# Forget gates and scaled keys made in the input projection instead of in the scan

## The chip, the cores and the metric

The kernel runs on one core of a Trainium2 chip. The metric is the device time of one launch in microseconds (us). A core has five engines with a queue each, worked off in order: TensorE (PE; its weight loads are listed apart as PEld), VectorE (DVE), ScalarE (ACT), GpSimd (POOL) and SyncE (SP, which here only issues DMAs). PSUM is the small memory into which TensorE writes; SBUF is the working memory.

## The reference

One layer of a bidirectional encoder over 1024 positions with 1024 channels, all in float32:

```python
h = rmsnorm(x)
proj = h @ w_in                       # 8192 columns
glu_in, q, v, z_f, z_b, og, g_a, g_b = split(proj)
a = silu(layernorm(dwconv31(glu(glu_in)))) @ pw_w
# the HGRN2 scan, once forward (z_f) and once backward (z_b), 8 heads of 128:
f   = lb + (1 - lb) * sigmoid(z)      # forget gate, then clipped to [1e-6, 1]
key = (1 - lb) * sigmoid(-z)
S_t = diag(f_t) S_{t-1} + key_t v_t^T ;  o_t = S_t^T (silu(q_t) * 128**-0.5)
b = (per-head rmsnorm(o_fwd + o_bwd) * silu(og)) @ o_w
x = x + (sigmoid(g_a) * a + sigmoid(g_b) * b) @ w_out
x = x + (silu(dwconv3(h2 @ w_gate)) * (h2 @ w_up)) @ w_down      # h2 = rmsnorm(x)
out = rmsnorm(x)
```

`lb` is a lower bound for each channel and direction, made from `lb_logits`.

## The kernel before

Everything is held transposed: channels on the 128 partitions, positions along the free dimension, in tiles of 128 x 512 ("half" 0 and 1 are the two halves of the sequence). Each float32 product is made of three matmuls on split operands (a high part and a rest, helper `split`, line 125: a cast on ScalarE, a subtraction on VectorE); these are lines 149 to 151. 

TensorE's order is written out by hand, as generators that are advanced piece by piece and woven into each other ("streams"). ScalarE, VectorE, GpSimd and SP get their order from a planner at compile time: it puts ready instructions out by program order under a model of time, and takes buffers of a tag from a pool of fixed size (`bufs`). Only instructions that are pinned keep the program's order. So a change in what the other engines do leaves TensorE's order as it is, and plans the other queues anew.

The parts that matter here, in the order of time:

1. **Input projection.** The columns of q, og, v, z_f, z_b, g_a and g_b are cut into heads of 128 (list `todo`, line 810). Two neighbours of the list are made by one `pair_job` (line 283), a seven-product form of a 2 x 2 block product: the products 1, 2, 6, 7, 5, 4, 3 follow each other on TensorE, 12 matmuls each, in PSUM banks "mm", "tr" and "sc". Products 1, 6 and 7 are copied out by ScalarE (line 440, tile `su`) and TensorE adds the next product but one to the same bank, so it waits for that copy. Four evacuations follow from the sums: for three of the four quadrants VectorE adds two sources (line 800), for the fourth ScalarE copies the bank (line 805); the result lands in an `ev` page (3 buffers) and SP stores it to DRAM (line 806). q and og also get a silu (line 803). Pairs 0 to 7 make q and og, pairs 8 to 18 make v, z_f and z_b of heads 0 to 6 and v of head 7: eight of these eleven pairs hold one z, and pairs 10, 13 and 16 hold z_f and z_b of one head. 19 pairs (`NPAIRS`) run here.
2. Woven into it, in this order: the depthwise convolution, 124 taps on VectorE (line 1039), and the layer norm in two halves (lines 1056 to 1083). Its squares (line 1071) take four `tm` pages at once, of which there are four; its matmuls (lines 1065, 611 and 601) stand in TensorE's order; its silu is line 1079.
3. **The scan.** 16 iterations (8 heads, two halves). `scan_inputs` (line 1152) loads q and the z of both directions and makes from each z the sigmoid of -z (tile `kG`, line 1163), the sigmoid (1164), the gate (1165) and, for both directions at once, the clip (1166). `scan_base` (line 1217) scales the keys (line 1224) and then multiplies keys and queries by products of gates over blocks of 1, 2, 4, ... positions (helper `tt`, line 1144; copies by `woven`, line 1176); `scan_levels` makes the matmuls between blocks (line 1281). The inputs of an iteration are asked for two iterations ahead.
4. TensorE's gaps in the scan are filled with the dense jobs (`rest_jobs`, line 1090): the columns that the 19 pairs leave over, which are z_f and z_b of head 7 (used by the last two iterations), g_a and g_b, and then the convolution's pointwise product. They evacuate through line 803 or 805.
5. Output projections and the feed-forward network follow.

`lbw` (line 981) holds lb and 1 - lb for each head and direction. `ev()` and `tmp()` give the next `ev` or `tm` page.

Of the kernel before, what the change touches and what calls it, by code (L numbers as in the profile page):

```python
# [10 lines left out]
F32 = mybir.dt.float32  # L11
# [3 lines left out]
AF = mybir.ActivationFunctionType  # L15
ALU = mybir.AluOpType
AX = mybir.AxisListType

P = 128
# [29 lines left out]
def tile_hybrid_encoder(  # L49
# [22 lines left out]
    nc = tc.nc  # L72
    PSUM = bass.MemoryType.PSUM
    V, A, G, T = nc.vector, nc.scalar, nc.gpsimd, nc.tensor
# [9 lines left out]
    NH = D // DK  # L84
    OFF_Q, OFF_V, OFF_ZF, OFF_ZB, OFF_OG, OFF_GA, OFF_GB = [2 * CW + i * D for i in range(7)]

    cp = ctx.enter_context(tc.tile_pool(name="const", bufs=1))
# [7 lines left out]
    def nm(s):  # L95
        uid[0] += 1
        return f"{s}_{uid[0]}"
# [3 lines left out]
    def bank(tag):  # L101
        return ps.tile([P, H], F32, tag=tag, name=nm(tag), bufs=BANKS[tag])

    def page(pool, tag, bufs, dt=F32):
        return pool.tile([P, H], dt, tag=tag, name=nm(tag), bufs=bufs)

    def tmp():
        return page(mp, "tm", 4)

    def ev():  # L110
        return page(mp, "ev", 3)
# [439 lines left out]
    def scratch(name, *dims):  # L551
        if not dims:
            return dp.tile([P, H], F32, name=name)
        return [scratch(f"{name}_{i}", *dims[1:]) for i in range(dims[0])]
# [7 lines left out]
    d_q = scratch("d_q", NH, 2)  # L562
    d_v = scratch("d_v", NH, 2)
    d_og = scratch("d_og", NH, 2)
    d_z = scratch("d_z", 2, NH, 2)
    d_bm = scratch("d_bm", NH, 2)
    d_x0 = dp.tile([P, 4, ND, P], F32, name="d_x0")
    d_xt = [[d_x0[:, :, k, :], scratch(f"d_xt_{k}")] for k in range(ND)]
# [227 lines left out]
    def store(dst, func=None):  # L796
        def evac(half, x0, x1=None, op=None):
            t = ev()
            if x1 is not None:
                V.tensor_tensor(t, x0, x1, op=op)  # L800
                x0 = t
            if func is not None:
                A.activation(t, x0, func)
            elif x1 is None:
                A.copy(t, x0)
            nc.sync.dma_start(dst[half], t)

        return evac

    todo = [  # L810
        t
        for h in range(NH)
# [7 lines left out]
        for h in range(NH)  # L820
        for t in (
            (OFF_V + h * DK, store(d_v[h])),
            (OFF_ZF + h * DK, store(d_z[0][h])),
            (OFF_ZB + h * DK, store(d_z[1][h])),
        )
    ]
    todo += [(OFF_GA + i * P, store(d_ga[i], AF.Sigmoid)) for i in range(ND)]
# [153 lines left out]
    lbw = cp.tile([P, 4, 2 * NH], F32, name="lbw")  # L981
# [6 lines left out]
    V.tensor_tensor(lbw[:, 2, :], lbw[:, 1, :], lbw[:, 1, :], op=ALU.subtract)  # L988
    V.tensor_scalar(lbw[:, 3, :], lbw[:, 2, :], -1.0, 1.0, op0=ALU.mult, op1=ALU.add)

    def lb_of(d, h):
        return lbw[:, 2, d * NH + h : d * NH + h + 1]

    def oml_of(d, h):
        return lbw[:, 3, d * NH + h : d * NH + h + 1]
# [143 lines left out]
    hp = tc.alloc_tile_pool(name="heads", bufs=1, reuse_waits="tile")  # L1139
# [3 lines left out]
    def tt(o, a, b, op=ALU.mult):  # L1143
        V.tensor_tensor(o, a, b, op=op)  # L1144

    kscale = cp.tile([P, 2 * NH], F32, name="kscale")
    V.tensor_scalar(kscale, lbw[:, 3, :], DK**-0.5, None, op0=ALU.mult)

    def c4(t):
        return t.rearrange("p (c t) -> p c t", c=4)  # L1150

    def scan_inputs(i):


        h, half = divmod(i, 2)
        q = page(hp, "q", 2)
        f = hp.tile([P, 2, H], F32, tag="f", name=nm("f"), bufs=2)
        kG = hp.tile([P, 2, H], F32, tag="kG", name=nm("kG"), bufs=3)
        nc.sync.dma_start(q, d_q[h][half])
        for d in range(2):  # L1160
            z = page(hp, "zi", 3)
            nc.sync.dma_start(z, d_z[d][h][half])
            A.activation(kG[:, d, :], z, AF.Sigmoid, scale=-1.0)
            A.activation(z, z, AF.Sigmoid)
            A.activation(f[:, d, :], z, AF.Identity, scale=oml_of(d, h), bias=lb_of(d, h))
        V.tensor_scalar(f, f, MIN_FORGET, 1.0, op0=ALU.max, op1=ALU.min)
        return q, f, kG, kscale[:, h : h + NH + 1 : NH]

    def pairs(t, h, other=H):

        return view(t, 0, [[other + h, 2], [2 * h, H // (2 * h)], [1, h]])

    def woven(t, h):

        t_h = page(hp, "A", 8)
        A.copy(pairs(t_h, h, 0), pairs(t, h))  # L1176
        return t_h

    def slot(b, n):
        return b[:, n * P : (n + 1) * P]  # L1180

    def near(t):
        return t.rearrange("p (c t) -> p c t", c=4)

    def over(m):
        return view(m, 0, [[0, 4], [1, 32]])
# [6 lines left out]
    def level(b, A_t, Q_t):  # L1193
        for at, g, o in each():
            T.matmul(b[g, o], A_t[:, at : at + 32], Q_t(at), start=True, stop=True)

    def row(t):
        return lambda at: t[:, at : at + 32]

    def double_keys(kG, tb, h):  # L1200
        n, nb = H // (2 * h), H // h
        tt(pairs(kG, h), pairs(kG, h), view(tb, 1, [[nb - 1, 2], [2, n], [0, h]]))

    def double_queries(qF, q, tb, h):
        n, nb = H // (2 * h), H // h
        tt(pairs(qF, h), q, view(tb, nb + 1, [[-(nb + 1), 2], [2, n], [0, h]]))

    def totals(tb, h, to=None):
        n, nb = H // (2 * h), H // h
        tn = None  # L1210
        if to is None:
            tn = hp.tile([P, 2, n], F32, tag=f"tb{h}", name=nm("tb"), bufs=1 if h < 8 else 2)
            to = view(tn, 0, [[n, 2], [1, n]])
        tt(to, view(tb, 0, [[nb, 2], [2, n]]), view(tb, 1, [[nb, 2], [2, n]]))
        return tn

    def scan_base(ins):


        q, f, kG, ks = ins  # L1220
        qF = hp.tile([P, 2, H], F32, tag="qF", name=nm("qF"), bufs=4)
        D_t = hp.tile([P, 4, 32], F32, tag="D", name=nm("D"), bufs=3)
        for d in range(2):
            V.tensor_scalar(kG[:, d, :], kG[:, d, :], ks[:, d : d + 1], None, op0=ALU.mult)
        k_d, Q1 = page(hp, "A", 8), page(hp, "A", 8)
        tt(k_d, kG[:, 0, :], kG[:, 1, :], ALU.add)
        A1 = woven(kG, 1)
        odd = H // 2
        tt(
            pairs(Q1, 1, 0),  # L1230
            view(q, 0, [[1, 2], [2, odd], [1, 1]]),
            view(f, H, [[1 - H, 2], [2, odd], [1, 1]]),
        )
        tt(
            view(qF, 1, [[H - 1, 2], [2, odd]]),
            view(q, 1, [[-1, 2], [2, odd]]),
            view(f, H + 1, [[-(H + 1), 2], [2, odd]]),
        )
        double_keys(kG, f, 1)
        double_queries(qF, pairs(Q1, 1, 0), f, 1)  # L1240
        tb = totals(f, 1)
        yield
        A2, Q2 = woven(kG, 2), woven(qF, 2)
        double_keys(kG, tb, 2)
        double_queries(qF, pairs(qF, 2), tb, 2)
        tb = totals(tb, 2)
        A4, Q4 = woven(kG, 4), woven(qF, 4)
        yield
        b = bank("sc")
        for n, (k_t, q_t) in enumerate(((k_d, q), (A1, Q1), (A2, Q2), (A4, Q4))):  # L1250
# [154 lines left out]
    class Base:  # L1405
        def __init__(self, ins):
            self.gen, self.val = scan_base(ins), None
# [39 lines left out]
    for h in range(NH):  # L1447
# [4 lines left out]
        for half in range(2):  # L1452
# [3 lines left out]
            ins = scan_inputs(i + 2) if i + 2 < NI else None  # L1456
# [17 lines left out]
            qF, kG = base[:2]  # L1474
# [556 lines left out]
```

## Time and profile before

| | |
|---|---|
| time, median of 3 runs | 1738.62 us (1736.96 to 1738.87) |
| profiled execution | 1740.57 us, its span 1738.7 us |
| granted TensorE clock | 0.997 |
| first store of z | 281.9 us |
| first load of z in the scan | 483.1 us |
| ScalarE table loads | 6 in the whole kernel, one of them (487.7 us) between 122 and 1093 us |

The profile page gives for each engine the time in which it was busy, as a sum and in 40 slices of the span (each 43.5 us, a digit is tenths). PEclk is the granted clock. Groups of instructions are named by line, engine and operation, with out<-in by the program's tile names, the shape and the count; durations are minimum/median/maximum in ns. Waits are told as "who waits <- for whom: us in total, times, longest". A timeline row has the start in us, the duration, and in brackets the idle time of the engine before it and what ended it.

### The profile page before, as it was taken

What the parts mean: (1) busy time and instruction counts of PE and PEld (TensorE: products, weight loads), DVE (VectorE), ACT (ScalarE), POOL (GpSimd) and SP (SyncE); (2) the same over time, 40 slices, a digit from 0 to 9 for tenths busy, and PEclk for the clock granted to TensorE, in tenths of its full rate; (3) what the DMA queues carried; (4) which work ended last, traced back from release to release, by engine and by line L of the source; (5) the groups of instructions that cost most, each with busy time, mean ns of one, the idle gap of its engine ahead of it and who ended that gap; (6) DMA issues with size and microseconds to landing.
All of it is one profiled execution on the core that took longest, in us unless ns stands there. A gap on an engine that the chain in (4) does not pass through costs nothing. (4 is left out here: it accounts for less than half of the span.)

```text
span 1738.7 us, 30440 instructions
## 1 busy us (share of the span) xinstructions
PE 1708.0 (98%) x11806; PEld 1408.5 (81%) x11806; DVE 1252.1 (72%) x1919; ACT 828.3 (48%) x1544; POOL 170.1 (10%) x184
## 2 busy tenths in 40 slices
PE   8999999999999999999999999999999999999997
PEld 6878888887888888888878887888887888888775
DVE  4599999746678888788556467676767776657864
ACT  7444433334476777776342245444334434443333
POOL 2211111100000000000000002011111111000110
PEclk9999999999999999999999999999999999999998
DMA  8768888854663444436579466577777876773842
GB/s 285 241 169 186 199 188 194 212 162 157 210 204 108 126 131 126 126 120 200 178 260 326 140 206 194 146 157 153 163 164 166 178 169 152 241 253 113 199 91 97
DMA packets 343750, 308.26 MB, mean 177 GB/s; under 512 B 25262, under 2 KB 255798, under 8 KB 343606
## 3 DMA queue, kind: packets, MB, share of 16 engines
q1 hardware_dynamic: 289590, 267.51, 48.8%
q0 software_dynamic: 44800, 37.76, 15.0%
q10 hardware_dynamic: 9216, 1.05, 0.4%
q8 instruction: 92, 1.51, 0.4%
q14 instruction: 52, 0.43, 0.1%
HBM read 201.40 MB, written 87.03 MB: 166 GB/s over the span
## 5 line engine op out<-in xcount | busy, mean ns | idle before, releaser
L149 PE MATMUL mm<-hx,wp 128*128 128x512 f32 x1068 | 427.6, 400 | 4.9 <-ACT su L440 2.1
L151 PE MATMUL mm<-hx,wp 128*128 128x512 f32 x1068 | 417.7, 391 | 1.0 <-DVE wp L125 0.8
L150 PE MATMUL mm<-hx,wp 128*128 128x512 f32 x1068 | 416.3, 390 | 0.5 <-DVE hx L125 0.5
L125 ACT CAST wp<-wr 128x1024 fp32r<-128x1024 f32 (+2 forms) x147 | 147.2, 1002 | 272.9 <-PE mm L150 108.0
L149 PEld LDWEIGHTS mm<-hx,wp 128*128 128x128 f32 x1068 | 200.6, 188 | 48.3 <-ACT su L440 3.2
L151 PEld LDWEIGHTS mm<-hx,wp 128*128 128x128 f32 x1068 | 200.4, 188 | 47.2 <-DVE wp L125 4.1
L150 PEld LDWEIGHTS mm<-hx,wp 128*128 128x128 f32 x1068 | 200.8, 188 | 40.9 <-DVE hx L125 1.7
L125 DVE TENSOR_TENSOR wp<-wr,wp 128x1024 fp32r<-128x1024 f32 (+2 forms) x145 | 169.2, 1167 | 84.1 <-ACT wp L125 77.7
L1039 DVE SCALAR_TENSOR_TENSOR acc<-gl,v_b,acc 128x1024 f32<-128x1024 f32 x120 | 148.7, 1273 | 0.4
L1144 DVE TENSOR_TENSOR qF<-qF,tb 128x512 f32<-128x512 f32 x96 | 65.0, 685 | 19.9 <-ACT A L1176 19.8
L440 ACT COPY su<-mm 128x512 f32<-128x512 f32 x82 | 47.5, 580 | 51.8 <-PE mm L151 51.7
L149 PE MATMUL tr<-hx,wp 128*128 128x512 f32 x180 | 70.5, 392 | 0.0
L151 PE MATMUL tr<-hx,wp 128*128 128x512 f32 x180 | 70.1, 389 | 0.0
L150 PE MATMUL tr<-hx,wp 128*128 128x512 f32 x180 | 70.0, 389 | 0.0
L1636 DVE SCALAR_TENSOR_TENSOR tm<-gp,v_a,tm 128x512 f32<-128x512 f32 x88 | 65.9, 749 | 3.8 <-ACT tm L1634 2.0
L125 ACT CAST wq<-sw 128x1024 fp32r<-128x1024 f32 x41 | 43.2, 1053 | 53.5 <-PE mm L150 42.6
L1144 DVE TENSOR_TENSOR kG<-kG,tb 128x512 f32<-128x512 f32 x96 | 65.2, 684 | 3.7 <-PE sc L1281 3.6
L149 PE MATMUL mm<-hy,wp 128*128 128x512 f32 x164 | 64.2, 391 | 0.0
L150 PE MATMUL mm<-hy,wp 128*128 128x512 f32 x164 | 63.8, 389 | 0.0
L150 PE MATMUL sc<-hy,wq 128*128 128x512 f32 x164 | 63.8, 389 | 0.0
L151 PE MATMUL mm<-hy,wp 128*128 128x512 f32 x164 | 63.8, 389 | 0.0
L151 PE MATMUL sc<-hy,wq 128*128 128x512 f32 x164 | 63.8, 389 | 0.0
(372 smaller groups left out, 3571.1 us busy)
## 6 DMA issues: line engine op xcount, KB each, us to landing
wr<-in_w_in_dram SPq DMA_DIRECT2D x48, 512.0 KB
wr<-in_ffn_w_up_dram SPq DMA_DIRECT2D x22, 512.0 KB
sw<-in_w_in_dram SPq DMA_DIRECT2D x38, 256.0 KB
d_g<-ft SPq DMA_DIRECT2D x38, 256.0 KB
sw<-in_ffn_w_up_dram SPq DMA_DIRECT2D x38, 256.0 KB
sw<-in_ffn_w_up_dram POOLq DMA_DIRECT2D x19, 512.0 KB, 8.0
wr<-sw POOLq DMA_DIRECT2D x32, 256.0 KB, 3.8
wr<-wr POOLq DMA_DIRECT2D x32, 256.0 KB, 4.2
```

The source lines that it names most:

```text
L125: parts = A.copy(hi, src), eng.tensor_tensor(lo, src, hi.bitcast(F32), op=ALU.subtract)
L149: T.matmul(acc, whi[:, k, :], ahi, start=first, stop=False, skip_group_check=again)
L150: T.matmul(acc, whi[:, k, :], alo, start=False, stop=False, skip_group_check=again)
L151: T.matmul(acc, wlo[:, k, :], ahi, start=False, stop=last, skip_group_check=again)
L440: A.copy(t, acc)
L1039: V.scalar_tensor_tensor(acc, g[:, k : k + S], tap(k), acc, op0=ALU.mult, op1=ALU.add)
L1144: V.tensor_tensor(o, a, b, op=op)
L1636: V.scalar_tensor_tensor(c, g[:, o + k : o + k + H], vec("fdw", k * NF + j), c, op0=ALU.mult, op1=ALU.add,)
```

## The change

`store_gates` takes the place of `store` for the z columns: after the evacuating addition (or straight from PSUM) it makes both sigmoids, scales the key with (1 - lb) / sqrt(128) on ScalarE, stores it, makes the gate, clips it on VectorE and stores it. DRAM holds `d_f` and `d_k` in place of `d_z`. `scan_inputs` only loads them, and `scan_base` no longer scales the keys. `kscale` is made earlier. TensorE's instructions and their order stay.

```diff
-    d_z = scratch("d_z", 2, NH, 2)
+    d_f = scratch("d_f", 2, NH, 2)
+    d_k = scratch("d_k", 2, NH, 2)
...
+    def store_gates(d, h):
+        def evac(half, x0, x1=None, op=None):
+            f, key = ev(), tmp()
+            if x1 is not None:
+                V.tensor_tensor(f, x0, x1, op=op)
+                x0 = f
+            A.activation(key, x0, AF.Sigmoid, scale=-1.0)
+            A.activation(f, x0, AF.Sigmoid)
+            A.activation(key, key, AF.Copy, scale=kscale_of(d, h))
+            nc.sync.dma_start(d_k[d][h][half], key)
+            A.activation(f, f, AF.Identity, scale=oml_of(d, h), bias=lb_of(d, h))
+            V.tensor_scalar(f, f, MIN_FORGET, 1.0, op0=ALU.max, op1=ALU.min)
+            nc.sync.dma_start(d_f[d][h][half], f)
+
+        return evac
...
-            (OFF_ZF + h * DK, store(d_z[0][h])),
-            (OFF_ZB + h * DK, store(d_z[1][h])),
+            (OFF_ZF + h * DK, store_gates(0, h)),
+            (OFF_ZB + h * DK, store_gates(1, h)),
...
         for d in range(2):
-            z = page(hp, "zi", 3)
-            nc.sync.dma_start(z, d_z[d][h][half])
-            A.activation(kG[:, d, :], z, AF.Sigmoid, scale=-1.0)
-            A.activation(z, z, AF.Sigmoid)
-            A.activation(f[:, d, :], z, AF.Identity, scale=oml_of(d, h), bias=lb_of(d, h))
-        V.tensor_scalar(f, f, MIN_FORGET, 1.0, op0=ALU.max, op1=ALU.min)
-        return q, f, kG, kscale[:, h : h + NH + 1 : NH]
+            nc.sync.dma_start(f[:, d, :], d_f[d][h][half])
+            nc.sync.dma_start(kG[:, d, :], d_k[d][h][half])
+        return q, f, kG
...
-        q, f, kG, ks = ins
+        q, f, kG = ins
...
-        for d in range(2):
-            V.tensor_scalar(kG[:, d, :], kG[:, d, :], ks[:, d : d + 1], None, op0=ALU.mult)
```

More of the change, by code (lines that the diff above doesn't have):

```diff
@@ L989, in tile_hybrid_encoder, with kscale_of @@
     V.tensor_scalar(lbw[:, 3, :], lbw[:, 2, :], -1.0, 1.0, op0=ALU.mult, op1=ALU.add)
+    kscale = cp.tile([P, 2 * NH], F32, name="kscale")
+    V.tensor_scalar(kscale, lbw[:, 3, :], DK**-0.5, None, op0=ALU.mult)
+    def kscale_of(d, h):
+        return kscale[:, d * NH + h : d * NH + h + 1]
     def lb_of(d, h):
@@ L1144, in tt @@
         V.tensor_tensor(o, a, b, op=op)
-    kscale = cp.tile([P, 2 * NH], F32, name="kscale")
-    V.tensor_scalar(kscale, lbw[:, 3, :], DK**-0.5, None, op0=ALU.mult)
     def c4(t):
```

## The prediction

> **What bounds the kernel now.** I read the page first, then the waits of TensorE, then the busy time of each engine in the stages that the change touches.
>
> ```profile
> span 1738.7 us, 30440 instructions
> PE 1708.0 (98%) x11806; PEld 1408.5 (81%) x11806; DVE 1252.1 (72%) x1919; ACT 828.3 (48%) x1544; POOL 170.1 (10%) x184
> PE   8999999999999999999999999999999999999997
> PEclk9999999999999999999999999999999999999998
> ```
>
> TensorE is busy for 98% of the span, at full clock but for the last slice. A change that leaves TensorE's work alone can take away only time in which TensorE waits, or add such time. All waits of TensorE that concern the two touched stages are these (columns: total us, times, longest):
>
> ```profile
> PE mm L149 <- ACT su L440: 2.9, 3, 1.6
> PE sc L1281 <- DVE qF L1144: 1.9, 2, 1.0
> PE mm L149 <- DVE ev L800: 0.9, 1, 0.9
> PE sc L1329 <- ACT kT L1322: 0.7, 1, 0.7
> ```
>
> The scan (lines 1281 and 1329) has 1.9 + 0.7 = 2.6 us of them. That is the ceiling of what the scan can give back. The stages one by one (length, then busy us of each engine with its count, clock, DMA share, GB/s):
>
> ```profile
> core 0: us, PE busy (x) PEld busy (x) DVE busy (x) ACT busy (x) POOL busy (x), PEclk, DMA share, GB/s
> 266.10:324.80 58.70, 57.70 (x254) 47.15 (x253) 58.11 (x56) 18.47 (x26) 9.98 (x9) 1.00 0.83 196
> 324.80:422.30 97.50, 97.50 (x432) 80.20 (x431) 47.87 (x57) 33.81 (x49) 6.31 (x7) 1.00 0.58 162
> 422.30:484.00 61.70, 60.92 (x268) 49.35 (x267) 43.93 (x64) 31.55 (x53) 2.27 (x3) 1.00 0.70 231
> 484.00:500.00 16.00, 16.00 (x72) 13.24 (x71) 10.00 (x18) 13.26 (x22) 0.00 (x0) 1.00 0.81 271
> 500.00:880.00 380.00, 377.29 (x5905) 316.87 (x5904) 297.70 (x651) 261.38 (x596) 14.66 (x16) 1.00 0.45 140
> ```
>
> The rows are pairs 8 to 10 of the projection (with the last convolution taps), pairs 11 to 15, pairs 16 to 18 (with most of the layer norm), the first dense jobs, and the scan. TensorE is full in all of them; the scan's loss is 380.00 - 377.29 = 2.7 us. VectorE is full up to 324.8; ScalarE has half its time free until 484 and is busy for 83% of 484 to 500.
>
> **The change part by part.** Durations come from one profiled execution of 1740.57 us (span 1738.7 and 1.9 around it); it is 0.11% above the median of 1738.62, on which I put the differences.
>
> ```profile
> L1163 ACT ACTIVATE kG<-zi x32: 614/634/660, 489.0 to 800.5; 128x512 f32<-128x512 f32 x32
> L1164 ACT ACTIVATE zi<-zi x32: 614/632/652, 490.1 to 801.3; 128x512 f32<-128x512 f32 x32
> L1165 ACT ACTIVATE f<-zi,lbw x32: 801/814/859, 491.1 to 802.1; 128x512 f32<-128x512 f32 x32
> L1166 DVE TENSOR_SCALAR f<-f x16: 677/693/695, 492.7 to 803.0; 128x1024 f32<-128x1024 f32 x16
> L1224 DVE TENSOR_SCALAR kG<-kG,kscale x32: 469/481/488, 489.7 to 801.1; 128x512 f32<-128x512 f32 x32
> L806 SPq DMA_DIRECT2D d_z<-ev x32: 319/328/1187, 281.9 to 508.8; - x32
> L1162 SPq DMA_DIRECT2D zi<-d_z x32: 319/320/1148, 483.1 to 774.2; - x32
> L440 ACT COPY su<-mm x82: 560/587/590, 116.7 to 1481.9; 128x512 f32<-128x512 f32 x82
> L805 ACT COPY ev<-mm x15: 565/579/582, 286.0 to 508.1; 128x512 f32<-128x512 f32 x15
> ```
>
> *Taken from the scan.* ScalarE loses 32 x (0.634 + 0.632 + 0.814) = 66.6 us, VectorE 16 x 0.693 + 32 x 0.481 = 26.5 us. TensorE gains from this only where it waited. One of the two waits on VectorE shows the cause:
>
> ```profile
> 757.57 0.69 DVE L1166 TENSOR_SCALAR f<-f 128x1024 f32<-128x1024 f32 x1 [0.22 <-ACT f L1165]
> 763.05 0.69 PE L1281 MATMUL sc<-qF,kG 128*64 128x64 f32 x16 [0.90 <-DVE qF L1144]
> ```
>
> The clip with the wait ahead of it takes 0.69 + 0.22 = 0.91 us of a VectorE queue that the matmul then awaits for 0.90. Without clip and scaling I count both of these waits as gone (-1.9) and the ScalarE one (0.7) as gone at even odds (-0.35): **-2.25**, between 0 (the new order of the queues puts others in their place) and -2.6.
>
> *Put into the projection.* 32 halves of z get one chain each: two sigmoids, a scaled copy and an affine step on ScalarE, a clip on VectorE, a second store. The chain is 0.63 + 0.63 + about 0.65 (bound by 0.587 without and 0.814 with two pointer operands) + 0.81 = 2.7 us when each waits for the last; back to back each starts some 0.1 sooner (below, two activations take 1.15), so 2.4. The 11 halves that leave PSUM through the plain copy (7 in pairs, 4 in dense jobs) save 0.58 each. ScalarE's sum is 32 x 2.4 - 11 x 0.58 = 70 us. A product of a pair lasts 2.72 us (97.50 us for 432 matmuls, 12 each), and a pair has seven. A pair with one z half-head has two chains, a pair with both directions (10, 13 and 16) four: 9.6 us of 19. With the 33.81 / 97.50 = 35% that ScalarE has there already, that is some 85% of such a pair and 60% of the others. Hence, outside the layer norm, no queue grows: what waits behind a chain is the copy of a product (line 440), which is due one product later: 2.72 - 0.59 = 2.1 us of room against a backlog of about 1. I cost it at nothing; if the chains came three in a row ahead of such a copy, each further 2.4 us would go straight to TensorE.
>
> *Layer norm on top (422 to 484).* Here is the price. ScalarE has 31.55 of 61.70 us; pairs 16 to 18 add 4 + 2 + 2 chains less two or three plain copies, about 18 us, and the tables change between silu (layer norm) and sigmoid. Together 31.55 + 18 + loads of about 5 is 55 of 61.7, and one wait is already here:
>
> ```profile
> 428.53 1.15 ACT L1079 ACTIVATE cx<-cx 128x512 f32<-128x512 f32 x2 [2.26 <-DVE cx L1078]
> ...
> 433.42 0.62 ACT L125 CAST ch<-cx 128x512 fp32r<-128x512 f32 x1
> 433.95 0.58 ACT L440 COPY su<-mm 128x512 f32<-128x512 f32 x1
> 434.58 0.50 PE L149 MATMUL mm<-hy,wq 128*128 128x512 f32 x1 [0.78 <-ACT su L440]
> 473.35 0.57 ACT L440 COPY su<-mm 128x512 f32<-128x512 f32 x1
> 475.72 0.59 ACT L440 COPY su<-sc 128x512 f32<-128x512 f32 x1 [1.28 <-PE sc L151]
> 478.89 2.66 ACT L125 CAST hx<-tm 128x512 fp32r<-128x512 f32 x4 [2.59 <-PE sc L150]
> ```
>
> A burst of silus and casts from 428.53 makes the copy, and TensorE behind it, late by 0.78. What a table load costs, the trace shows at 30.7 us:
>
> ```profile
> 30.48 0.22 ACT L750 ACTIVATION_READ_ACCUMULATOR junk<-xt 128x1 f32 x1
> 30.72 1.28 ACT L851 ACT_TABLE_LOAD   x1
> 32.02 0.60 ACT L851 ACTIVATE tm<-mm 128x512 f32<-128x512 f32 x1
> 117.32 1.28 ACT L985 ACT_TABLE_LOAD   x1
> 119.48 0.22 ACT L985 ACTIVATE lbw<-su 128x16 f32<-128x16 f32 x1 [0.88 <-DVE su L984]
> ```
>
> 1.28 us, with nothing before or after it. The load at 117.32 ran ahead of a wait and so was hidden, so a load in front of the burst costs 0 to 1.28; I take **+1.3**, since the queue is full there. The pair's four chains then end about 0.3 behind the room of the next pair's first copy: **+0.3** (0 to 3). At 475.72 the copy of a product would stand behind one chain and one load that begin after 473.9: 473.9 + 1.28 + 2.4 + 0.5 = 478.1 instead of 476.3; it is due 2.72 after its product ended, at 475.7 + 2.7 = 478.4. Shifted by the burst's own load it is 1.0 late: **+1.1** (0 to 3.7, one chain and one load). The casts at 478.89 have 2.59 of idle time ahead that covers them; if that is gone they push the second halves of the first dense jobs by what exceeds it.
>
> [...]
>
> *VectorE and PSUM.* 28 clips of half the size of line 1166 (0.35 to 0.48) go into the projection, eight of them ahead of 324.8 where VectorE is full and where the evacuation of line 800 already holds TensorE up once by 0.9: **+0.4**, one clip (0 to 1.8, half of them in the way). Elsewhere it is half idle and they cost nothing. The plain-copy halves keep their bank for two sigmoids, 0.5 us longer; "mm" has three banks and the next product uses another, so nothing.
>
> *DMAs and queues.* 32 more stores and 32 more loads of 256 KB. Eight more stores to 324.8 are 2.1 MB in 58.7 us, 36 GB/s on 196 with a share of 0.83, still under 1; later there is more room. SP issues 64 more at 0.33 us (21 us over 600). A store waits in SP's queue for its chain, and weight loads wait behind it, by 2 to 3 us; these loads run a pair, 19 us, ahead. In the scan f and the keys come straight from DMA; an iteration lasts some 23 us (380 / 16), a load is issued an iteration ahead, so nothing; the start of the scan loses the three activations between load and first multiply and loads twice as much, which I set against each other. POOL's queue is not passed.
>
> **Sum:** -2.25 + 1.3 + 0.3 + 1.1 + 0.4 = +0.85 us, +0.9 us or 0.05%: 1738.62 + 0.9 = 1739.5.
>
> **The rivals.** *Slower: the queue of ScalarE overflows in the layer norm.* The place is 422 to 484. The four "tm" buffers now hold key tiles as well, and the four squares of the layer norm need all four at once; ScalarE stands at 55 of 61.7 us. From a backlog of 2.1 us on (the room of a product's copy), every further microsecond is TensorE's. A backlog of 5 us in each half of the layer norm gives 2 x (5 - 2.1) = 5.8 us, to the other terms: +6.7, 1745.3; with 8 us in each, +12.7, 1751. For it: the wait of 0.78 at 434.58 without any of the new work. Against it: 6 us of free time over the stretch, and stores that nobody awaits.
>
> [...]
>
> *Faster: the scan gives more than its waits.* If the denser queues also slow TensorE between the waits that the profile names, relieving ScalarE of 66.6 of 261 us and VectorE of 26.5 of 298 could return more: all 2.7 us of the scan's loss, the 0.9 and 0.8 in the projection through another order, and about as much again unseen: -4.4 to -6, 1733 to 1734. For it: nothing but that ends of matmuls are modelled. Against it: PEld is 316.87 / 380 = 83% in the scan and 80.20 / 97.50 = 82% where nothing waits, so the scan is as tight as the rest. [...]
>
> *Nothing is moved in effect:* the planner puts chains into idle time and the scan's waits stay: 0 to +1, inside my forecast.
>
> **How the numbers follow.** About 0.2% (3.5 us) is what a measurement of this kernel can tell from no change. My sum with its bounds stays inside this in 0.49. The overflow has 0.32 and counts as slower; the drain has 0.06, and lies on the border, I count it slower too. Faster has 0.13. The likeliest case's own range is 1736 to 1742. The range for 8 in 10 leaves out half of the faster case and the far end of the overflow: 1735 to 1750.
>
> **What would show it.** Right: TensorE's waits at line 1281 on VectorE gone or halved; five ScalarE table loads between 270 and 490 where there was one; ScalarE over 85% in 422 to 484 and some 17 us less per 100 in the scan; TensorE's waits on line 440 grown by 2 to 4 us in that stretch, nothing new in pairs 9 to 15. Wrong: waits of TensorE on the layer norm's matmuls (lines 611 and 601), which would be the buffers' doing; waits on weights (line 125), which would be SP's queue; or new waits in the scan or after it, where a new order of the queues would have done what I did not foresee.

## The result, and the profile after

The change makes the kernel slower: 1757.01 us (median of 4 runs, 1756.31 to 1758.77) against 1738.74 us for the kernel before in 4 runs alongside, a ratio of 1.0101 with a 95% interval of 1.0087 to 1.0115. The forecast of 1739.5 and its range, up to 1750, missed it. The profiled execution took 1757.49 us, its span 1755.7, which is 17.0 more than before.

The page of the kernel after, its head, TensorE's slices and its clock:

```profile
span 1755.7 us, 30563 instructions
PE 1715.3 (98%) x11806; PEld 1412.7 (80%) x11806; DVE 1242.1 (71%) x1903; ACT 850.4 (48%) x1569; POOL 172.5 (10%) x184
PE   8999999999999999999999999999999999999997
PEclk9999999999999999999999999999999999999999
```

At this resolution almost nothing has moved: the span is 17.0 longer and TensorE, with the same 11806 matmuls, is busy 7.3 longer. The stages show where. The five rows answer to the five stage rows of the prediction (pairs 8 to 10, 11 to 15, 16 to 18, first dense jobs, scan; each bound is moved by what the same matmul is late there). The others, behind the "...", follow the granted clock, which is the first number behind the five busy times:

```profile
267.84:328.72 60.88, 59.01 (x254) 48.39 (x253) 57.70 (x59) 34.19 (x50) 10.02 (x9) 0.97 0.85 201
328.72:434.21 105.49, 101.43 (x432) 82.57 (x431) 55.76 (x73) 61.76 (x96) 6.31 (x7) 0.97 0.67 196
434.21:500.69 66.48, 61.82 (x268) 49.10 (x267) 44.05 (x68) 51.96 (x83) 2.23 (x3) 1.00 0.63 211
500.69:521.46 20.77, 17.73 (x72) 12.93 (x71) 13.70 (x23) 13.98 (x23) 0.00 (x0) 1.00 0.93 303
521.46:901.46 380.00, 376.96 (x5906) 317.12 (x5905) 274.38 (x606) 217.84 (x516) 16.95 (x16) 1.00 0.52 165
...
98.00:102.00 4.00, 4.00 (x12) 3.14 (x11) 3.39 (x6) 1.51 (x3) 0.75 (x5) 0.57 0.31 104
314.00:315.00 1.00, 1.00 (x3) 0.77 (x3) 1.00 (x2) 0.26 (x1) 0.43 (x1) 0.50 0.49 100
422.70:430.00 7.30, 7.25 (x22) 6.05 (x23) 2.08 (x3) 2.23 (x5) 1.24 (x2) 0.53 0.10 36
```

The four stages ahead of the scan last 253.6 us with 1026 matmuls; before, the same matmuls took 233.9 us. The loss is there: 19.7 us. In the scan ScalarE gave up 261.38 - 217.84 = 43.5 us and VectorE 297.70 - 274.38 = 23.3, and TensorE's idle time went from 2.7 to 3.0.

TensorE's waits in the stages ahead of the scan, and its largest of the scan (from the waits of the whole run):

```profile
PE mm L149 <- ACT su L440: 4.9, 4, 1.9
PE ob L612 <- DVE tm L1076: 2.8, 1, 2.8
PE mm L149 <- ACT hx L125: 1.8, 2, 0.9
PE ob L602 <- ACT tm L601: 1.8, 1, 1.8
PE ob L1088 <- DVE tm L1076: 1.1, 2, 0.9
PE mm L150 <- DVE hx L125: 1.1, 3, 0.7
...
PE sc L1295 <- DVE qF L1167: 2.9, 4, 1.3
```

These six make 13.5 us, where before there were 0.9 + 0.8 = 1.7: 11.8 of the 19.7. The other 8 us are TensorE being busy for longer with the same work. Most of that is the clock: in the profile after it stood at 0.50 for three windows of 3.4 us within these stages (one from 313.6, two from 422.8), each counted, by that clock, as half a window's work lost: 3 x 1.7 = 5.1 us. The rest, about 3, is not taken apart here; the first matmuls after the waits are a part of it (0.5 to 0.6 us instead of 0.39 in the rows below).

TensorE executes the same matmuls in the same order in both kernels, so the start of the same matmul can be compared in two traces. Against before, in us gained or lost in each stage (worked out from the two traces; minus is faster):

| | until 262 us | pairs 8-10 | 11-15 | 16-18 | first dense | scan | after it |
|---|---|---|---|---|---|---|---|
| after | +1.9 | +2.6 | +7.6 | +4.8 | +4.8 | -0.2 | -3.5 |

The second and the third column meet just ahead of the wait that opens pair 11, so they differ from the rows above by 0.4 us. The layer norm's first matmul (line 1065, at 405 us before) lies inside the third: up to it 3.4 us are lost, 2.6 and 0.8, and the other 6.8 of the 7.6 are lost behind it, most of them at the wait on line 612 and by the slow clock that follows.

The two outer columns have nothing in them that this change or an experiment edits on purpose. In the single profiled executions of this study they move, the first between -0.4 and +2.2, the last between -3.5 and +2.1 with one exception told below; only the columns between are read in what follows.

**Five places in the trace.** From the timeline of after, in this order: pair 10 (303 to 314), a table switch in the layer norm (443 to 448), its squares (419 to 423), its spread matmul (476 to 481), and the first dense job (506):

```profile
303.32 0.86 POOL L302 DMA_DIRECT2D wr<-wr  x1 [7.13 <-DMA wr<-sw]
309.50 1.05 ACT L125 CAST wp<-wr 128x1024 fp32r<-128x1024 f32 x1 [5.50 <-DMA wr<-wr]
310.45 0.59 ACT L817 ACTIVATE tm<-mm 128x512 f32<-128x512 f32 x1
312.73 0.58 ACT L440 COPY su<-mm 128x512 f32<-128x512 f32 x1
313.37 0.60 PE L149 MATMUL mm<-hy,wp 128*128 128x512 f32 x1 [1.87 <-ACT su L440]
...
443.70 1.05 ACT L125 CAST wp<-wr 128x1024 fp32r<-128x1024 f32 x1
444.77 1.28 ACT L817 ACT_TABLE_LOAD   x1
446.06 0.63 ACT L817 ACTIVATE tm<-ev 128x512 f32<-128x512 f32 x1
446.60 0.57 ACT L440 COPY su<-mm 128x512 f32<-128x512 f32 x1
447.22 0.50 PE L149 MATMUL mm<-hy,wq 128*128 128x512 f32 x1 [1.50 <-ACT su L440]
...
418.58 0.80 ACT L821 ACTIVATE ev<-ev,lbw 128x512 f32<-128x512 f32 x1
421.14 0.63 ACT L1094 ACTIVATE tm<-cx 128x512 f32<-128x512 f32 x1 [0.24 <-DVE tm L1074]
422.75 1.39 PE L612 MATMUL ob<-ones_m,tm 128*128 128x1 f32 x6 [2.80 <-DVE tm L1076]
...
476.32 0.39 ACT L601 ACTIVATE tm<-ident,r 128x128 f32<-128x128 f32 x1
479.87 0.98 ACT L601 ACTIVATE tm<-ident,r 128x128 f32<-128x128 f32 x3
480.90 1.13 PE L602 MATMUL ob<-tm,ones_m 128*128 128x512 f32 x2 [1.80 <-ACT tm L601]
...
506.26 0.62 ACT L125 CAST hx<-tm 128x512 fp32r<-128x512 f32 x1 [2.56 <-DMA tm<-d_h]
506.93 0.50 PE L149 MATMUL mm<-hx,wp 128*128 128x512 f32 x1 [0.95 <-ACT hx L125]
```

For the sums of weight blocks that a pair's seven products need, GpSimd issues DMAs that add in SBUF (line 302), and ScalarE casts the result (line 125). ScalarE reaches the cast of the next such weights at 303.99 (the cast before it, at 303.37, takes 0.62) and waits 5.50 us at the head of its queue until the sum has landed; the chain of a z tile is queued behind it, and the product's copy (440) behind the chain. TensorE waits 1.87. The same two places before:

```profile
299.58 0.86 POOL L302 DMA_DIRECT2D wr<-wr  x1 [4.16 <-DMA wr<-sw]
305.32 1.06 ACT L125 CAST wp<-wr 128x1024 fp32r<-128x1024 f32 x1 [3.07 <-PE mm L150]
```

There the first addition had come back after 4.16 us of GpSimd's waiting and not 7.13, and the cast did not wait for a DMA at all, but for a free weight page. A wait of the same kind, 1.00 us, stands at 335: the cast waits 1.41 us for its sum, and the rest of one chain and a whole second one stand between it and the copy.

The second group of rows is the layer norm's table switches: the load for the sigmoid at 444.77 puts the copy of a product 1.28 us back and TensorE waits 1.50. There are five such loads between 270 and 490, at 283.22, 438.23, 444.77, 484.06 and 489.63. The third is the squares (line 1094), and here two things meet. The first square starts at 416.93; then ScalarE works through the rest of a chain (818, 819, 821, from 417.45 to 419.38) and a product's copy, and the next two squares start at 419.75. The last waits 0.24 us for a `tm` page. The sums (1076) and the matmul on them (612) follow, and TensorE waits 2.80 us. These rows do not part the shortage of pages from the chain in the queue; e10 and e15 below take up one each. The fourth is plain queueing: four small activations for one spread matmul (601) begin at 476.32 and end only at 480.85, because the rest of a chain (818, 819, 821), a weight cast and a plain copy were planned in between. The last rows are the reloads of h for the first dense jobs. Their issues in the view of line 118, after and before:

```profile
L118 SPq DMA_DIRECT2D tm<-d_h x4: 320/402/494, 500.5 to 507.6; - x4
```

```profile
L118 SPq DMA_DIRECT2D tm<-d_h x4: 320/382/552, 466.6 to 470.3; - x4
```

They too go into `tm` pages. Before, all four were issued by 470.3; now the first only at 500.5 and the last at 507.6, while TensorE wants the results from 506 on.

### The profile page after: what moved, and what is told of

Same layout as the page of the kernel before. It is cut to its first block, busy times and chain, and to the rows that moved or that the text cites. A ratio compares the mean times of both kernels' runs of the same rounds, so it can differ in the third digit from the quotient of the medians.

```text
span 1755.7 us, 30563 instructions
## 1 busy us (share of the span) xinstructions
PE 1715.3 (98%) x11806; PEld 1412.7 (80%) x11806; DVE 1242.1 (71%) x1903; ACT 850.4 (48%) x1569; POOL 172.5 (10%) x184
## 3 DMA queue, kind: packets, MB, share of 16 engines
q10 hardware_dynamic: 9216, 1.05, 0.4%
## 5 line engine op out<-in xcount | busy, mean ns | idle before, releaser
L440 ACT COPY su<-mm 128x512 f32<-128x512 f32 x82 | 47.5, 579 | 43.5 <-PE mm L151 43.5
```

Source lines behind the costliest of these rows:

```text
L440: A.copy(t, acc)
```

## The experiments

Each row has the ratio to the kernel before, whose runs were taken on the same chip, and the losses against before by stage as above:

| run | ratio [95%] | pairs 8-10 | 11-15 | 16-18 | first dense | scan |
|---|---|---|---|---|---|---|
| after | 1.0101 [1.0087, 1.0115] | 2.6 | 7.6 | 4.8 | 4.8 | -0.2 |
| e4_scan_side | 0.9983 [0.9969, 0.9997] | 0.0 | 0.0 | -0.1 | 0.0 | -0.7 |
| e9_scale_gpsimd | 1.0031 [1.0018, 1.0043] | 0.2 | 0.1 | 0.0 | 0.0 | 6.2 |
| e6_stores_twice | 1.0015 [0.9996, 1.0035] | -0.3 | 4.1 | -0.1 | 0.0 | 0.6 |
| e2_heads_0_3 | 1.0022 [1.0003, 1.0041] | 0.6 | 5.0 | 0.0 | 0.0 | 0.0 |
| e3_heads_4_7 | 1.0064 [1.0044, 1.0083] | 0.1 | 4.8 | 4.7 | 4.1 | -0.5 |
| e7_no_silu_table | 1.0106 [1.0079, 1.0132] | -0.5 | 11.3 | 5.2 | 4.6 | -0.4 |
| e1_key_pages | 1.0126 [1.0098, 1.0154] | 8.4 | 3.1 | 12.3 | 0.0 | -0.2 |
| e8_gpsimd | 1.0191 [1.0162, 1.0221] | 4.8 | 16.4 | 12.8 | 5.9 | -0.8 |
| e10_tm_relief | 1.0071 [1.0048, 1.0095] | -0.4 | 6.9 | 5.6 | 0.0 | -0.2 |
| e11_sums_on_dve | 1.0059 [1.0035, 1.0082] | -0.9 | 7.1 | 6.4 | 6.7 | -0.1 |
| e12_all_reliefs | 1.0023 [1.0009, 1.0037] | -1.1 | 1.0 | 6.6 | 0.0 | 0.1 |
| e15_short_chain_alone | 1.0065 [1.0041, 1.0089] | -1.0 | 4.0 | 3.1 | 3.4 | -0.6 |
| e14_short_chain | 1.0030 [1.0014, 1.0047] | -1.2 | 2.6 | 2.5 | 0.0 | -0.8 |

The theory after reading the two traces: the loss is made ahead of the scan by ScalarE's chains standing in line before work that TensorE awaits, by keys that take the four `tm` pages, and by later weight sums. The rivals: only one of these counts, or the extra stores do it by traffic alone. Every edit below also has the queues planned anew, so a run shows what its edit and the new order do together.

### The scan without the work, and nothing put elsewhere

```diff
-            z = page(hp, "zi", 3)
-            nc.sync.dma_start(z, d_z[d][h][half])
-            A.activation(kG[:, d, :], z, AF.Sigmoid, scale=-1.0)
...
+            nc.sync.dma_start(f[:, d, :], d_q[h][half])
+            nc.sync.dma_start(kG[:, d, :], d_og[h][half])
```

> The scan's side of the change alone, on the kernel before: the projection stores z as before, and the scan loads two finished tiles for each direction (those of q and og stand in for gates and keys, so the recurrence is computed on other data) with no sigmoid, affine step, clip or scaling. My prediction: the waits at line 1281 go, -1.9 to -2.6 us, 1736.4. Rival: the queues of the scan are planned anew and put others in their place, 0 (1738.7), as the changed kernel's 2.9 us of such waits suggest.

The small matmuls of the scan (the two times ahead of the form are the first and the last start) and the wait that stands first in this run's list; below it the same matmuls before:

```profile
L1191 PE MATMUL sc<-q,A x512: 196/196/217, 502.6 to 833.0; 128*32 128x32 f32 x171
...
PE sc L1275 <- DVE qF L1144: 2.3, 3, 1.1
```

```profile
L1195 PE MATMUL sc<-q,A x512: 196/196/217, 502.8 to 833.9; 128*32 128x32 f32 x171
```

From the first to the last of these it is 330.4 us against 331.1. So the scan takes 0.7 us less in all, nearer to the rival's 0 than to the expected 1.9 to 2.6, and the wait on VectorE's block products, which the prediction counted as gone, is still there and larger: without clip and scaling the planner gives another order, and another product is late. The median is 2.95 us below before; only 0.7 of it is in the scan, and the profile puts the rest behind the scan, where nothing was changed. Whether that rest is real stays open.

### Key scaling on GpSimd, in the kernel before

```diff
-            V.tensor_scalar(kG[:, d, :], kG[:, d, :], ks[:, d : d + 1], None, op0=ALU.mult)
+            G.tensor_scalar(kG[:, d, :], kG[:, d, :], ks[:, d : d + 1], None, op0=ALU.mult)
```

> The kernel before with only the scaling of the keys in the scan (line 1224) moved from VectorE to GpSimd: 15 us less on VectorE, whose lateness is what TensorE waits for in the scan (1.9 us). If this were a way to beat the kernel before: -1 to -2 us, 1737. If GpSimd's time per instruction (some 1 us or more) is in the path of the keys: new waits, 1740 or more.

The scaling among the groups of instructions by line (busy us, mean ns, idle before):

```profile
L1224 POOL TENSOR_SCALAR kG<-kG,kscale 128x512 f32<-128x512 f32 x32 | 54.3, 1702 | 265.7 <-ACT kG L1163 115.9 <-DVE tb L1144 101.3 <-DVE D L1259 29.1
```

One scaling takes 1702 ns there and 481 on VectorE. The scan loses 6.2 us, as the second expectation said: its chain from load to matmul is sensitive to a step made longer, though taking the step away returned 0.7. What is free in the scan is free only up to its due time.

### The stores alone

```diff
             nc.sync.dma_start(dst[half], t)
+            if twice is not None:
+                nc.sync.dma_start(twice[half], t)
```

The kernel before, with z stored a second time.

> The kernel before with each z stored a second time to DRAM: 32 more stores of 256 KB from the same page, and no other work. Theory C: the weight sums that run through DRAM-to-SBUF additions land later, the cast behind them waits, and TensorE loses what it lost in pairs 10 and 11 (4.8 us), 1743. Theories A and B: the stores alone cost nothing, 1738.7 within 1.5.

The median is 1.8 us above before, less than half of what theory C asked for, and the interval includes no change. The profiled execution has 4.1 us in pairs 11 to 15, among them a wait of 1.80 at 325.5 on an evacuation of VectorE and one slow window (from 327.35 to 330.34 the matmuls start 0.43 us apart and not 0.23), and nothing in the layer norm or later. Stores and the new order that they bring can cost something in pairs 8 to 15, but they are no cause of the loss in pairs 16 to 18 and in the dense jobs.

### The change for half of the heads

```diff
-            (OFF_ZF + h * DK, store_gates(0, h)),
-            (OFF_ZB + h * DK, store_gates(1, h)),
+            (OFF_ZF + h * DK, store_gates(0, h) if h < 4 else store(d_z[0][h])),
+            (OFF_ZB + h * DK, store_gates(1, h) if h < 4 else store(d_z[1][h])),
```

and the scan's inputs accordingly; the second run has `h >= 4`.

> Gates and keys of heads 0 to 3 are made in the projection (pairs 8 to 13), those of heads 4 to 7 in the scan as before. If the loss comes from meeting the layer norm (A and B alike), only the waits in pairs 10 and 11 stay (4.8 us) and the time is 1743 to 1744. If chains cost anywhere in the projection, half of the loss stays, about 1748. If the new order of the queues as such is at fault, no value is more likely than another.

> The other half: heads 4 to 7 in the projection (pairs 14 to 18 and the first two dense jobs), heads 0 to 3 in the scan as before. If the loss comes from meeting the layer norm and the start of the dense jobs, 18.3 less 4.8, that is 1752. If it is spread evenly, 1748. With the run of heads 0 to 3 the two differences should add up to about 18 if the places act for themselves.

The first half loses 0.22%, in the profile all of it in pairs 8 to 15, with waits of 1.2 at 311 and 3.6 at 334 on the product's copy. The second loses 0.64%, and shows the layer norm's and the dense jobs' waits as after does (2.8 on line 612's counterpart, 1.8 on 602's). Together 0.86% of the 1.01%: the loss belongs to places, and it is larger where the chains meet the layer norm.

### No table switch in the layer norm

```diff
-            A.activation(xn, xn, AF.Silu)
+            A.activation(sg, xn, AF.Sigmoid)
+            V.tensor_tensor(xn, xn, sg, op=ALU.mult)
```

> The changed kernel, but the layer norm's silu is made as x times sigmoid(x), with the product on VectorE, so that ScalarE stays on one table from the first z on: four loads of 1.28 us fewer. Theory B: the waits at 447 (1.7) and 492 (0.7), each behind two loads, go, and later ones shrink, 1752 to 1754.5. Theory A: 1757, as the pages are held as long as before. My prediction's term for these loads was 1.3 + 1.1 us.

Where the loads stood, the waits went: the 1.50 at 447 is gone, and so is one of 0.49 at 492. The ratio did not move (1.0106 against 1.0101). In this order of the queues there are a 3.3 at 334 with two slow windows behind it (the granted clock was 0.57 from 333 to 341) and 2.0 at line 1088 in their place. So the loads cost what is seen at their places, 1.50 and 0.49, where the prediction had 1.3 and 1.1; but taking them away alone, for a product more on VectorE, gained nothing.

### Other pages for the keys

```diff
-            f, key = ev(), tmp()
+            f, key = ev(), key_page()
```

`key_page` takes the convolution's pages once they are free.

> The changed kernel, but the key tiles get pages of their own (in the projection the free pages of the convolution's input, in the scan the pages that held z before) and no longer take one of the four tm pages. Theory A, the buffers: the layer norm's squares (four tm pages at once) and the four reloads of h ahead of the first dense jobs wait for keys that are on their way to DRAM; then the waits of TensorE at 422 to 425 us (5.6 with the slow clock after it), 462 (0.6) and 506 to 513 (4.8) go and 1757.0 becomes about 1746. Theory B, ScalarE's queue: the same chains stand ahead of the same copies, and only the reloads at 506 get earlier, 1752 or more. Theory C, the DMAs: nothing changes, 1757.

Its two largest waits of TensorE, and one row of VectorE's timeline:

```profile
PE mm L149 <- ACT su L440: 7.4, 3, 5.4
PE mm L149 <- DVE ev L801: 7.3, 1, 7.3
...
305.32 0.69 DVE L1082 TENSOR_TENSOR tm<-cx 128x512 f32<-128x512 f32 x1 [6.23 <-DMA cx<-d_cv]
```

The waits on lines 612 and 1088 and those of the dense jobs are gone, as the pages' theory says; the kernel is slower all the same. From 299.1 to 305.3 VectorE sits for 6.23 us on a sum of the layer norm that waits for its load (last row, of the timeline), with an evacuation queued behind it that TensorE awaits for 7.33, until 309: the planner had pulled that sum forward, it seems because `tm` pages were free. The 5.4 us that end at 451 stand behind silus and their casts, a table load that waits 0.56 us for one of the new pages, a chain and the first step of the next; and the wait on line 602 grew from 1.8 to 3.0. So this run frees the pages and shows their places healed, but it can't give the price of the pages.

### Two steps of the chain on GpSimd

```diff
-            A.activation(key, key, AF.Copy, scale=kscale_of(d, h))
+            G.tensor_scalar(key, key, kscale_of(d, h), None, op0=ALU.mult)
...
-            A.activation(f, f, AF.Identity, scale=oml_of(d, h), bias=lb_of(d, h))
+            G.tensor_scalar(f, f, oml_of(d, h), lb_of(d, h), op0=ALU.mult, op1=ALU.add)
```

> The changed kernel, but the scaling of the key and the affine step of the gate are made by GpSimd in place of ScalarE: the chain keeps two of four instructions on ScalarE, some 32 x 1.35 = 43 us less there. Theory B: the waits behind chains shrink by half, 1757 to about 1749. Theory A: pages are held longer as GpSimd is slower, 1757 or more. GpSimd also issues the weight sums of pairs 8 to 13, so its queue could delay these: then pairs 9 to 13 lose more than 4.8.

The two steps among the groups of instructions by line (out<-in, count, busy, mean ns, idle before):

```profile
L819 POOL TENSOR_SCALAR tm<-tm,kscale 128x512 f32<-128x512 f32 x32 | 65.7, 2079 | 119.0 <-ACT tm L817 116.6 <-DMA d_f<-ev 2.5
L821 POOL TENSOR_SCALAR ev<-ev,lbw 128x512 f32<-128x512 f32 x32 | 33.5, 1047 | 0.0
```

On ScalarE these took 0.71 and 0.81; here 2.08 and 1.05, in the queue that also issues the weight sums. ScalarE is relieved, and the two steps take 3.13 us and not 1.52. That pages and PSUM banks are held for longer by this, and the weight sums issued later, is the author's inference and not shown. It loses twice as much as the change. The relief of ScalarE's busy time did not help where the length of the chain and GpSimd's queue grew; the run cannot part these two.

### Pages only: squares and reloads elsewhere

```diff
-        sqs = [tmp() for _ in xs]
+        sqp = [gp0.tile([P, 2, H], F32, tag="gl", name=nm("sq"), bufs=NCW) for _ in range(NCW // 2)]
+        sqs = [sqp[j // 2][:, j % 2, :] for j in range(NCW)]
...
-        t = load(d_h[k][1])
+        t = two[:, k % 2, :]
+        nc.sync.dma_start(t, d_h[k][1])
```

Here the keys stay in `tm`, and the work that they displace gets the convolution's pages.

> The changed kernel with the other users of the four tm pages moved off them, and the keys left on them: the layer norm's four squares and the four reloads of h ahead of the dense jobs use the free pages of the convolution's input. Theory A (buffers): the wait at line 612 with the slow clock after it (5.6), the one at 462 and the ones of the first dense jobs (4.8) go, 1757 becomes 1746 to 1748, with no new wait since nothing of the chains waits for these pages. Theory B (ScalarE's queue, chains ahead of the squares): only the reloads gain, 1752.

Its largest wait ahead of the scan, and that place in the timeline:

```profile
PE mm L149 <- ACT su L440: 7.5, 4, 4.3
...
330.80 1.05 ACT L125 CAST wp<-wr 128x1024 fp32r<-128x1024 f32 x1 [3.88 <-DMA wr<-wr]
335.98 0.80 PE L149 MATMUL mm<-hy,wp 128*128 128x512 f32 x1 [4.26 <-ACT su L440]
```

The 2.80 at line 612 and all of the dense jobs' 4.8 us are gone. The expected 1746 to 1748 was missed all the same (the ratio puts it at 1751): the wait at 335, 1.00 after, is 4.26, again with a weight cast that waits for a DMA at the head of ScalarE's queue, and the matmuls behind it start 0.43 us apart and not 0.23 up to 339.99 at least. The ratio is 1.0071: of what the pages cost, part came back elsewhere. From the layer norm's first matmul to the scan the profiled execution loses 6.1 us, where after loses 16.3.

### Weight sums on VectorE

```diff
-            first=n == 0 or n >= 14,
+            first=n == 0 or n >= 11,
```

From pair 11 on, and not from 14, VectorE adds the weight blocks.

> The changed kernel with the weight sums of pairs 11 to 13 made by VectorE, as those of pairs 14 to 18 are, in place of additions by DMA that GpSimd issues. Theory C for pairs 10 to 12: a cast of ScalarE waits for such a sum, the chain and the copy of a product wait behind it; without these sums the waits at 313 and 335 (4.8 us with the slow clock) go, 1752. If the chains themselves are at fault there, the waits stay, and VectorE, which is full up to 331 us, adds its own.

No cast of ScalarE waits for a sum there any more, and the waits at 313 and 335 shrink from 1.9 and 1.0 to one of 0.61 at 330; line 612's 2.8 and the dense jobs' waits stay. The ratio of 1.0059 has an interval that lies below that of after. Its profiled execution was the slowest of its four. In it the 3.4 us that after loses up to the layer norm's first matmul are gone (-0.4), but the stages behind lose more than after's (the granted clock of the whole execution was 0.993, after's 0.994), so the gain of the median is not seen there.

### The three reliefs together

e10, e11 and e7 in one kernel.

> The three causes taken away together: tm pages relieved, weight sums of pairs 11 to 13 on VectorE, no silu table in the layer norm. If the causes are the right ones and add up, 4.8 + 11 + 2.4 of 18 us go, and the time is that of the kernel before, 1739 to 1742. If something else is behind the loss, it stays above 1748.

The two largest of TensorE's waits ahead of the scan:

```profile
PE ob L1088 <- DVE tm L1076: 2.8, 2, 2.6
PE ob L602 <- ACT tm L601: 1.8, 1, 1.8
```

The ratio falls to 1.0023: three quarters of the loss go when the three are taken away together, and some 4 us stay. What is left is in pairs 16 to 18: two waits of the layer norm's matmuls, and a slow window after one of them (the granted clock was 0.99 from 262 to 505 us). Why these still come late this run doesn't show.

### A shorter chain

```diff
-            A.activation(f, x0, AF.Sigmoid)
+            V.tensor_scalar(f, key, noml_of(d, h), 1.0, op0=ALU.mult, op1=ALU.add)
...
-            A.activation(f, f, AF.Identity, scale=oml_of(d, h), bias=lb_of(d, h))
```

The gate is made from the other sigmoid, f = 1 - (1 - lb) sigmoid(-z), on VectorE: two activations for each chain and not four. Once on the change alone, once on top of the three reliefs.

> The changed kernel with only the shorter chain. Theory A (pages): the waits of the squares and of the first dense jobs stay, about 10 of 18 us, the rest shrinks: 1.0060 of before. Theory B (ScalarE's queue alone): all waits halve or better, 1.0040 or less. Theory C (weight sums by DMA): pairs 10 to 12 keep a wait, as the cast still waits for its sum, but the copy of the product stands behind two instructions and not four: 1 to 2 us less there.

> The run with all three reliefs, and the gate made from the key's sigmoid by one VectorE instruction (1 - (1 - lb) sigmoid(-z)), so that ScalarE has two instructions of each chain instead of four, some 45 us less, and VectorE one more. Theory B for what is left: the waits at the layer norm's matmuls (1.8 at line 602, 2.6 at line 1088 with 1.7 of slow clock) go, and the time comes to that of the kernel before within 0.1%. If the pages are behind them, they stay, 1.0023.

Of the first, these waits of TensorE ahead of the scan:

```profile
PE mm L149 <- ACT su L440: 2.8, 3, 2.1
...
PE ob L612 <- DVE tm L1081: 1.0, 1, 1.0
PE ob L602 <- ACT tm L601: 0.6, 1, 0.6
```

Alone it takes the loss ahead of the scan from 19.8 to 9.5 us; line 612's wait falls from 2.8 to 1.0, 602's from 1.8 to 0.6, the copies' from 4.9 to 2.8, and every stage loses less. At pair 10 a cast still waits 5.21 us for its sum, as theory C says, and TensorE no longer waits behind it. So the length of ScalarE's chain is a cause too, with the sums as late and the pages as short as they were. It is not one at every place: the copy behind the table load waits 2.1 us and not 1.5. The ratio of 1.0065 is near theory A's 1.0060 and not theory B's 1.0040: the chain is not the only cause. On top of the reliefs 602's wait falls likewise from 1.8 to 0.6, and the stages lose 3.9 and not 6.5, but the median is not better (1.0030, against 1.0023, and the intervals overlap), and the expected 0.1% is missed. A wait of 2.6 us at 324 on an evacuation by VectorE, which has one more instruction for each chain, is new. The profiled execution, 6 us above the median of its run, lost 7.7 us after the scan, where nothing was edited, among other waits one of 2.7 on a copy at line 440. That loss isn't explained.

No kernel of the study is faster than the one before except e4, which makes no gates.

## Why the prediction was wrong, point by point

**The scan, -2.25.** Wrong in size. Measured 0.2 (after), 0.6 to 0.8 (e15, e4, e14). The step that failed is that a wait "counts as gone" when the instruction named ahead of it goes. VectorE's queue was ordered anew, and 2.9 us of waits of the same kind stand there after. The prediction named this as its lower bound, 0.

**"Outside the layer norm, no queue grows", "I cost it at nothing".** Wrong by 3.4 us, which is what pairs 8 to 15 lose ahead of the layer norm's first matmul. The room of 2.1 us was set against an average backlog. But ScalarE works in order, and a cast that waits for a late weight sum (5.50 us at 304) holds the chain and the copy behind it whatever the queue's average load. ScalarE's load was 61.76 of 105.49 in pairs 11 to 15, 59%, near the 60% that was predicted for most pairs. It takes both, the late sum and the long chain: e11 has the sums out of the way, e15 has a shorter chain behind a sum as late, and neither loses anything there (-0.4 and 0.0).

**"These loads run a pair, 19 us, ahead", DMAs at nothing.** Wrong for one kind. TensorE was not held up by SP's loads but by GpSimd's sums by DMA, which came later (GpSimd waited 7.13 us for the first of two and not 4.16), and they were not on the list. That the extra traffic made them late is argued from e6 and from the DMA share (0.83 to 0.85), not shown; that their lateness costs is shown by e11, for pairs 8 to 15 ahead of the layer norm.

**The layer norm, +2.7, and the casts at 478.89 "covered".** This is the step that cost most: from the layer norm's first matmul to the scan 16.3 us are lost, and not 2.7. ScalarE's load was no more than foreseen, 51.96 us in pairs 16 to 18 against 55. The table loads came as drawn, five of 1.28 us, two of them felt (1.50 at 447, 0.49 at 492), and e7 removed just these. The copies late by one load are the part that was right. What the sum had at nothing was the keys' hold on the four `tm` pages: it stood in the rival alone, with "stores that nobody awaits" against it. Squares late by 2.80, the spread by 1.80, and the reloads of h, which moved from 466 to 500; the 2.59 of idle time that should have covered the casts covered nothing, since the loads themselves came late. With the pages out of the way (e10) the first and the last are gone, 6.1 of the 16.3 us stay, and among them the spread's 1.80. The chain's length is the other part: with pages as short as in after and a shorter chain (e15) some 9 stay, and the spread's wait is 0.6.

**The clip, +0.4.** The evacuation that VectorE delayed by 0.9 before no longer appears in the list of waits ahead of the scan: another order, and no loss.

**The rivals.** The overflow in the layer norm named the place (422 to 484), the `tm` pages and the lines to look at (601 and 611, now 602 and 612), and had 0.32, so the right account was there as the second choice; its price of 6.7 to 12.7 was too low, since its place was too short (line 612's wait falls at 414 of before, and pages still cost 4.8 in the dense jobs) and knew nothing of the clock. "The drain", to which the prediction gives 0.06, would be a stop of ScalarE at a table load beyond the load itself; no run shows one: the load at 444.77 ends at 446.05 and the sigmoid starts at 446.06, with the cast before it ending at 444.75. "Faster" and "nothing moved" fell with the result.

**The slow clock** appears in no step of the prediction. It is 5.1 of the 19.7 us (10.2 us at a granted clock of 0.50).

**The sum as it should have been**, ahead of the scan: waits 11.8, clock 5.1, restarts and the rest 3; the scan -0.2.

## What to carry to other kernels

Work moved off an engine with slack pays only if TensorE waited for that engine (in the scan 43.5 us less of ScalarE and 23.3 less of VectorE gave 0.2), and waits named in a profile mostly change their owner when the queues are ordered anew; work moved onto an engine with 40% idle time can still stop TensorE, when it stands in an in-order queue between a late DMA and a copy that TensorE needs (ScalarE was busy for 34.19 of 60.88 us in pairs 8 to 10, where a cast waited 5.50 us and TensorE then 1.87). Before calling a move free, list for its new place what shares its buffers, what is queued behind it, and the one instruction ahead of it that may block. And look at the clock behind a wait of TensorE: here waits of 1.87 and 2.23 us were each followed by 3.41 us at a granted clock of 0.50, 1.7 us more, and waits of 1.50 and 1.80 us in the same kernel were not.

## What the runs showed of the hardware that was not expected

After three single waits of TensorE in the kernel after, of 2.23, 1.87 and 2.80 us, its granted clock stood at 0.50 for 3.41, 3.41 and 6.83 us. The waits that precede the slow window at 98 after, and the same matmul before, where no slow window followed:

```profile
97.42 0.50 PE L149 MATMUL mm<-hx,wp 128*128 128x512 f32 x1 [2.23 <-ACT tm L868]
```

```profile
97.07 0.50 PE L149 MATMUL mm<-hx,wp 128*128 128x512 f32 x1 [1.45 <-ACT tm L851]
```

After 2.23 us here, 1.87 at 313 and 2.80 at 422 the granted clock fell to 0.50 (the rows of 98, 314 and 422.7 above); after 1.50 at 447 and 1.80 at 481 it did not. While it was at 0.50 the matmuls followed each other at 0.427 us and not 0.227, so 3.41 us cost 1.7 by the clock and 1.6 by this spacing, and 6.83 us in a row (422.84 to 429.67) twice as much. So among waits of 1.5 to 2.2 us some cost nearly as much again and some nothing.

What decides it the runs do not show. In the kernel after the slow stretches begin at 98.58, 313.62 and 422.84, which are 63 and 32 times 3.413 us apart, and last 3.41, 3.41 and 6.83 us. In the 3.41 us ahead of these starts TensorE sat idle for 2.23, 1.87 and 2.80 us. From 477.46 to 480.87 it sat idle for 1.77 us, and the clock stayed at 1.00. In other runs it went both ways: behind the wait of 1.80 us at 325.5 in e6 came a slow window, and behind the one of 2.6 us at 324 in e14 none (the granted clock was 1.00 from 262 to 505). So the length of a wait alone does not decide.
